# 1444 one-element memsets on GpSimd in a planned decoder-layer kernel

## The chip, the cores and the metric

The kernel runs on one core of a Trainium2 chip. The metric is the device time of one execution in microseconds (us). A core has a matrix engine (TensorE, PE in the profile, its weight loads PEld), VectorE (DVE), ScalarE (ACT), GpSimd (POOL) and SyncE (SP), which here only issues transfers. Each engine works through its own list of instructions in order and waits on semaphores for the others; 16 DMA engines move the data.

## The reference, cut to what matters

One mixer layer runs on 1024 new tokens and on 8 single tokens with stored state, at model width 2048:

```
h = rmsnorm(x) * (1 + scale(c)) + shift(c)          # modulation from w_ada
z = h @ w_in                                        # 2048 x 8208
y_a = b * conv3(c_a * h_a) * silu(g_a)              # 8 groups of 128 channels
q, k, v = silu(conv4(qkv)); q, k = l2norm(q), l2norm(k)
o = gated_delta_rule(q, k, v, g, beta, s0)          # 8 heads of 128, chunked, triangular solve
y = concat(y_a, rmsnorm(o) * silu(g_b)) @ w_out     # 2048 x 2048
out = final_rmsnorm(x + gate(c) * y)
```

The outputs also hold the new convolution and delta-rule states. The delta rule is sequential: each head's state S goes from one chunk of tokens to the next. Nothing in the reference corresponds to a memset.

## The kernel before

**Work.** The tokens go in two halves: half 0 has 512 tokens, half 1 has 512 and the 8 single ones (520 columns in two blocks). Per half, w_in is walked in 64 column tiles of 128 (32 for the eight heads, 32 for the eight convolution groups) and then w_out in 16. A tile is four splits; a split is 512 rows by 128 columns of weights, `raw`. To keep fp32 precision at the faster fp32r matmul, `split_w` (L568) makes two parts of it: `whi`, a rounded copy by ScalarE, and `wlo = raw - whi`, by GpSimd or VectorE. The activations are split likewise (`hh`, `hl`; `yhi`, `ylo` for the output projection). Each 128 rows take three matmuls per block: hh with whi, hl with whi, hh with wlo. I call these matmuls, written to the tiles `mm`, the stream; one split is 12 of them per block. `raw`, `whi` and `wlo` have four buffers each.

**Side chains.** Beside the stream runs one chain per head and half (`gdn_prep`, `gdn_invert`, `gdn_apply`): transposes `tpt`, products of k and q (`sp`), a triangular solve by VectorE in 31 steps (`ob`, `xb`) with trips through memory (`ub`, `tb`, `xd`, `yc`), and then a row of small dependent products on TensorE, with a step on VectorE or ScalarE between each and the next: `cht<-xc,dU`, `cht<-yc,pt`, `cht<-X,dU`, `cht<-Y,pb`, `cht<-v,Y`, and for each of four token chunks `cht<-u,kt`, `ot<-u,dA`, `cht<-st,kq`, `cht<-rt,Y`. I call these the chain's steps.

**What sets the order.** Python code writes out each engine's list at build time. A planner (`_Order`) keeps an estimate of when each engine is free and each tile ready; every instruction issued through the wrappers `V`, `S`, `G`, `SY` and `mm` adds to it, GpSimd memsets too (L347: a cost of 0.035 plus 0.00085 per element in the planner's own units, and a claim on a port shared with VectorE in `shared`, L146). After every stream matmul `pump` (L247) asks which chains' next step has become ready in that estimate, and writes it there. So an instruction that is added anywhere can move steps everywhere behind it. Two rules matter here. In `split_w`, a split goes to GpSimd if the planner has GpSimd free within 1.0 of now, else to VectorE. And in `head` (L1680), a new head's first tile may not start before the chain of the head before the last has finished its last chunk:

```
if part == 0:
    while recd[half] < len(queue) - 2:
        od.advance()
```

`advance` (L255) writes no stream matmul: it moves the planner on to the next chain step and writes that. What it writes stands in TensorE's list with nothing of the stream between. I call such a place a hold. (The cause is memory: `kq`, a head's k and q, has three buffers.)

The split before the change:

```
def split_w(raw, whi, wlo):
    S.activation(whi[:], raw[:], AF.Copy)
    eng = G if od.free["G"] <= od.now + 1.0 else V
    eng.tensor_tensor(wlo[:], raw[:], whi[:].bitcast(F32), ALU.subtract)
```

Nearly all instructions go through the wrapper and carry its line L321 in the profile (L370 for matmuls), so they are told apart by tile names. `spot`, new, is one element in one partition; L454 to L459 of the changed file are part of the setup, behind the memsets of `ones`, `nhalf`, `phalf` and `sc` on GpSimd and ahead of that of `wlt`.

Of the kernel before, what the change touches and what calls it, by code (L numbers as in the profile page):

```python
# [8 lines left out]
F32 = mybir.dt.float32  # L9
# [68 lines left out]
def trunk_kernel(tc, xT, w_in, w_ada, w_out, pack, consts, vecs, csq, ssm,  # L78
                 yT, cap, cqp, ssp, cas, cqs, sss):
    nc = tc.nc  # L80
    ctx = ExitStack()
    with ctx:
        _trunk(ctx, tc, nc, xT, w_in, w_ada, w_out, pack, consts, vecs, csq, ssm, yT, cap, cqp, ssp, cas, cqs, sss)
# [299 lines left out]
def _trunk(ctx, tc, nc, xT, w_in, w_ada, w_out, pack, consts, vecs, csq, ssm, yT, cap, cqp, ssp, cas, cqs, sss):  # L383
    od = _Order()
    V, S, G, SY = (_Engine(od, e, k) for e, k in ((nc.vector, "V"), (nc.scalar, "S"), (nc.gpsimd, "G"), (nc.sync, "Y")))
    mm, pump = _Tensor(od, nc.tensor).mm, od.pump

    def pool(name, bufs, stack=ctx, **kw):
        return _Pool(od, stack.enter_context(tc.tile_pool(name=name, bufs=bufs, **kw)), bufs)

    RAW, SPL, FX = 4, 4, 5
    cp = pool("cp", 1)
# [34 lines left out]
    def pkv(n, a=0, w=None):  # L427
        o, ww = PK[n]
        return pk[:, o + a:o + a + (ww if w is None else w)]

    def ck(n, a=0, w=None):
# [22 lines left out]
    V.tensor_tensor(sc[:, :, 0:9], cth[:, :144].rearrange("p (k b) -> p k b", b=9),  # L454
                    pkv("c").rearrange("p (k b) -> p k b", b=9), ALU.mult)

    held = {"ch": 0}


# [108 lines left out]
    def split_w(raw, whi, wlo):  # L568
        S.activation(whi[:], raw[:], AF.Copy)
        eng = G if od.free["G"] <= od.now + 1.0 else V  # L570
        eng.tensor_tensor(wlo[:], raw[:], whi[:].bitcast(F32), ALU.subtract)

    class Stream:

# [28 lines left out]
        def ahead(self, most=SPL):  # L603

            while True:
                if self.loaded < min(self.split + RAW, len(self.todo)):
                    raw = wp.tile([P, 4, P], F32, tag="raw", name="raw", bufs=RAW)
                    for a, b, src in self.todo[self.loaded][1]:
                        SY.dma_start(raw[:, a:b, :], src)
                    self.raws.append(raw)  # L610
                    self.loaded += 1
                elif most and self.split < min(self.freed + SPL, self.loaded) and (
                        self.eager or self.split < self.used + 2 or self.landed()):
                    whi = wp.tile([P, 4, P], F32R, tag="whi", name="whi", bufs=SPL)
                    wlo = wp.tile([P, 4, P], F32R, tag="wlo", name="wlo", bufs=SPL)
                    split_w(self.raws[self.split], whi, wlo)
                    self.raws[self.split] = None
                    self.done.append((whi, wlo))
                    self.split += 1
                    most -= 1  # L620
                else:
                    return
# [1293 lines left out]
```

## Time and profile before

| what | value |
|---|---|
| median of 3 runs | 2313.4 us (2312.58 to 2316.38) |
| the profiled execution | 2316.31 us |
| its span, first to last instruction | 2314.5 us |
| mean granted TensorE clock | 0.965 |
| TensorE busy | 2165.6 us (94%) |
| VectorE busy | 1236.9 us (53%) |
| ScalarE busy | 827.1 us (36%) |
| GpSimd busy | 827.3 us (36%), 807 instructions |

The profile is of one execution, which took 1.8 us beyond its span and 2.9 us more than the median. Times in it count from the span's start. Matmuls overlap, so a busy TensorE may still be slowed: by the granted clock, which is 1.0 or 0.5 at any moment, and shows as a mean in each stretch. A row of the timeline has start, duration, engine, line, operation, tiles written and read, shapes, count, and in brackets how long the engine stood idle before and for whom.

### The profile page before, as it was taken

Reading aid. Unit: us, or ns where it says so; the run is one execution under the profiler, and the core shown is the slowest. Engines: PE = TensorE matmul, PEld = TensorE weight load, DVE = VectorE, ACT = ScalarE, POOL = GpSimd, SP = SyncE. Lnnn points to the kernel's source line nnn. Section 1 sums busy time; section 2 is a strip of 40 time slices with the busy share of each in tenths; the row PEclk is TensorE's granted clock in tenths of the full one; section 3 lists DMA queues with packets and bytes.
Section 4 is the critical chain, followed back from the end, with each engine's and each line's share of the span. In section 5 each row is a group of like instructions: output and inputs, shape, how many; then the busy total and the mean of one; then the engine's idle time right before and its main releaser. Section 6 shows DMA issues by size and latency. Waiting matters only on the chain. (4 is left out here: it accounts for less than half of the span.)

```text
span 2314.5 us, 38944 instructions
## 1 busy us (share of the span) xinstructions
PE 2165.6 (94%) x14297; PEld 1867.5 (81%) x14297; DVE 1236.9 (53%) x3647; ACT 827.1 (36%) x1885; POOL 827.3 (36%) x807
## 2 busy tenths in 40 slices
PE   5999999897989999789999999998989999999997
PEld 2467677675868888568889999998989998898996
DVE  3355676463856662148315757655465476235545
ACT  3234243333434323133324334242433432225553
POOL 1223433333324334222434333343433342334444
PEclk8999999998979999989999999999999999999998
DMA  9965977997656667976445786679894565997776
GB/s 323 328 173 87 155 148 131 121 132 101 128 76 88 95 92 77 58 114 190 151 120 100 129 106 105 122 98 95 99 88 83 87 95 87 77 68 211 211 222 202
DMA packets 462496, 299.56 MB, mean 129 GB/s; under 512 B 37600, under 2 KB 421344, under 8 KB 462304
## 3 DMA queue, kind: packets, MB, share of 16 engines
q1 hardware_dynamic: 438512, 284.26, 71.2%
q10 hardware_dynamic: 23792, 12.81, 2.2%
q8 instruction: 112, 1.84, 0.3%
q14 instruction: 80, 0.66, 0.1%
HBM read 277.06 MB, written 19.94 MB: 128 GB/s over the span
## 5 line engine op out<-in xcount | busy, mean ns | idle before, releaser
L321 POOL TENSOR_TENSOR wlo<-raw,whi 128x512 fp32r<-128x512 f32 x535 | 710.3, 1330 | 1377.8 <-ACT whi L321 1234.8
L370 PE MATMUL mm<-hh,whi 128*128 128x264 f32 (+1 forms) x3008 | 982.1, 326 | 33.3 <-ACT whi L321 17.5
L370 PE MATMUL mm<-hh,wlo 128*128 128x264 f32 (+1 forms) x3008 | 982.2, 327 | 10.3 <-POOL wlo L321 9.3
L370 PE MATMUL mm<-hl,whi 128*128 128x264 f32 (+1 forms) x3008 | 978.2, 325 | 1.4 <-DVE hl L321 1.4
L321 ACT ACTIVATE whi<-raw 128x512 fp32r<-128x512 f32 x672 | 418.5, 628 | 769.0 <-DMA raw<-in_w_in 312.1
L370 PEld LDWEIGHTS mm<-hh,whi 128*128 128x128 f32 x3008 | 576.2, 192 | 91.2 <-ACT whi L321 23.4
L370 PEld LDWEIGHTS mm<-hh,wlo 128*128 128x128 f32 x3008 | 576.2, 192 | 63.3 <-POOL wlo L321 18.0
L370 PEld LDWEIGHTS mm<-hl,whi 128*128 128x128 f32 x3008 | 576.4, 192 | 45.0 <-issue 3.4
L370 PE MATMUL mm<-yhi,wlo 128*128 128x512 f32 (+2 forms) x768 | 250.0, 326 | 5.6 <-DVE wlo L321 4.4
L370 PE MATMUL mm<-ylo,whi 128*128 128x512 f32 (+2 forms) x768 | 249.0, 324 | 2.8 <-DVE ylo L321 2.7
L370 PE MATMUL mm<-yhi,whi 128*128 128x512 f32 (+2 forms) x768 | 248.5, 324 | 0.9 <-ACT whi L321 0.9
L321 DVE TENSOR_TENSOR ob<-tb,xb 128x62 f32<-128x62 f32 (+30 forms) x992 | 196.3, 238 | 24.3 <-DMA tb<-ub 24.2
L321 DVE TENSOR_TENSOR wlo<-raw,whi 128x512 fp32r<-128x512 f32 x137 | 105.4, 775 | 162.8 <-ACT whi L321 159.8
L321 DVE TENSOR_TENSOR xb<-xb,ob 128x62 f32<-128x62 f32 (+30 forms) x992 | 184.4, 226 | 0.0
L370 PEld LDWEIGHTS mm<-yhi,wlo 128*128 128x128 f32 x768 | 146.6, 191 | 20.0 <-DVE wlo L321 6.0
L370 PEld LDWEIGHTS mm<-ylo,whi 128*128 128x128 f32 x768 | 146.6, 191 | 16.8 <-DVE ylo L321 4.1
L370 PEld LDWEIGHTS mm<-yhi,whi 128*128 128x128 f32 x768 | 146.6, 191 | 12.6 <-ACT whi L321 1.3
L321 DVE SCALAR_TENSOR_TENSOR kq<-zr,pk,kq 128x512 f32<-128x512 f32 x96 | 100.1, 1043 | 3.4
L321 DVE SCALAR_TENSOR_TENSOR res<-mm,ga,xr 128x512 f32<-128x512 f32 (+2 forms) x48 | 27.3, 568 | 111.5 <-PE mm L370 103.8
L321 DVE TENSOR_TENSOR acc<-acc,sqt 128x512 f32<-128x512 f32 (+3 forms) x70 | 50.1, 719 | 46.8 <-ACT sqt L321 45.8
L321 DVE TENSOR_SCALAR u<-cht,sm 128x128 f32<-128x128 f32 x64 | 22.3, 348 | 71.3 <-PE cht L370 71.3
L321 DVE SCALAR_TENSOR_TENSOR rt<-cht,gt_neg,v 128x128 f32<-128x128 f32 x56 | 19.5, 349 | 67.8 <-PE cht L370 67.6
(408 smaller groups left out, 1981.8 us busy)
## 6 DMA issues: line engine op xcount, KB each, us to landing
raw<-in_w_in SPq DMA_DIRECT2D x488, 256.0 KB, 7.0
raw<-in_w_out SPq DMA_DIRECT2D x160, 256.0 KB, 3.1
wat<-in_w_ada SPq DMA_DIRECT2D x64, 512.0 KB, 7.2
gw<-in_w_ada SPq DMA_DIRECT2D x64, 256.0 KB, 7.9
tb<-ub ACTq DMA_DIRECT2D x16, 512.0 KB, 8.3
raw<-in_w_in SPq DMA_DIRECT2D x48, 128.0 KB, 6.4
sl<-in_ssm SPq DMA_DIRECT2D x12, 512.0 KB, 6.2
x1s<-in_xT SPq DMA_DIRECT2D x16, 260.0 KB, 8.1
```

The source lines that it names most:

```text
L321: r = f(*args, **kw)
L370: r = self.pe.matmul(out, lhsT, rhs, **kw)
```

## The change

The change adds a tile of one element, 100 memsets of it during setup and two more behind each of the 672 splits, all on GpSimd, 1444 in all. Nobody reads the tile. They are issued through the planner's wrapper `G`.

```
+    spot = cp.tile([1, 1], F32, name="spot")
+    for _ in range(100):
+        G.memset(spot[:], 0.0)
...
     def split_w(raw, whi, wlo):
         S.activation(whi[:], raw[:], AF.Copy)
         eng = G if od.free["G"] <= od.now + 1.0 else V
         eng.tensor_tensor(wlo[:], raw[:], whi[:].bitcast(F32), ALU.subtract)
+        for _ in range(2):
+            G.memset(spot[:], 0.0)
```

**On GpSimd.** In the rows below, from the start of GpSimd's list after the change, "waits Pool_49" is a wait on GpSimd's own semaphore: every memset of `spot` but the first waits for an earlier one of them, since they write the same element. The other waits are on transfers (DMAHW), TensorE and ScalarE.

```order
L321 MEMSET sc 128x512
L321 MEMSET spot 1x1
L321 MEMSET spot 1x1 [waits Pool_49] x99
L321 MEMSET wlt 128x96
L321 ISA
L321 TENSOR_TENSOR rsm<-rsm,nhalf 128x4 [waits DVE_49]
L321 TENSOR_TENSOR wlo<-raw,whi 128x512 [waits DMAHW7_49,DMAHW0_49,Activation_49]
L321 MEMSET spot 1x1 [waits Pool_49] x2
L321 TENSOR_TENSOR wlo<-raw,whi 128x512 [waits DMAHW2_49,DMAHW1_49,Activation_49]
L321 MEMSET spot 1x1 [waits Pool_49] x6
```

Before, the memset of `wlt` follows that of `sc` directly, and splits follow each other. Groups of four, six or eight `spot` are those of splits whose subtraction went to VectorE. GpSimd subtracts 535 splits before and 520 after, VectorE 137 and 152.

**On TensorE, in half 0.** The stream of half 0 before the output projection is counted here in matmuls to `mm`. Behind the 1760th, at the boundary between two tiles, stands a hold before the change. The numbers behind names only tell buffers apart.

```order
L370 MATMUL mm<-hl,whi 128x512
L370 MATMUL mm<-hh,wlo 128x512
L370 MATMUL cht<-X,dU 64x64 x4
L370 MATMUL cht<-Y,pb 64x64 x4
L370 MATMUL cht<-v,Y 128x128
L370 MATMUL cht<-u_6057,kt 128x128
L370 MATMUL ot<-u_6059,dA 128x128
L370 MATMUL cht<-st_165,kq 128x128 x2
L370 MATMUL cht<-rt,Y 128x128
```

So it goes on, through all four chunks of this chain and the normalisation of half 1's input (`cht<-ones,acc` and `cht<-cs,rsm`), for 21 rows, until `ot<-u_6218,dA`; only then comes the next `mm<-hh,whi`. The same chain after the change, on the same engine:

```order
L370 MATMUL cht<-X,dU 64x64 x4
L370 MATMUL tpt<-sp 128x256 x6
L370 MATMUL mm<-hh,whi 128x512
L370 MATMUL mm<-hl,whi 128x512
L370 MATMUL mm<-hh,wlo 128x512
L370 MATMUL cht<-Y,pb 64x64 x4
L370 MATMUL mm<-hh,whi 128x512
L370 MATMUL mm<-hl,whi 128x512
L370 MATMUL mm<-hh,wlo 128x512
L370 MATMUL mm<-hh,whi 128x512
L370 MATMUL mm<-hl,whi 128x512
L370 MATMUL mm<-hh,wlo 128x512
```

The chain now begins at the 1668th stream matmul instead of the 1740th (`cht<-xc,dU`), and its steps stand mostly six stream matmuls apart; only its last, an `ot<-u,dA`, still stands at the 1760th, two behind the step it depends on.

The place at the 1568th, also a tile boundary, has one step before the change (`ot<-u,dA`). After it, TensorE's list reads:

```order
L370 MATMUL mm<-hl,whi 128x512
L370 MATMUL mm<-hh,wlo 128x512
L370 MATMUL cht<-rt,Y 128x128
L370 MATMUL cht<-u_5886,kt 128x128
L370 MATMUL ot<-u_5888,dA 128x128
L370 MATMUL mm<-hh,whi 128x512
L370 MATMUL tpt<-cs,kq 128x128 x4
```

Three dependent steps stand there in a row: a short hold. Over the whole program, steps that stand nearer than about five full-width stream matmuls to the step they depend on number 29 of 248 before (13 of them in the hold at the 1760th) and 18 of 248 after. The steps of a chain elsewhere are moved by up to some 200 stream matmuls, earlier or later; TensorE has the same instructions in all, and the output projections' stream is the same. SyncE issues the same transfers, most of them at the same place or one to three loads of weights away, and at most 17 (one `dA`).

## The prediction

> **What bounds the kernel now.** I read the page's first parts, then a table of stretches, then TensorE's timeline where it stalls, then the waits.
>
> ```profile
> span 2314.5 us, 38944 instructions
> ...
> PE 2165.6 (94%) x14297; PEld 1867.5 (81%) x14297; DVE 1236.9 (53%) x3647; ACT 827.1 (36%) x1885; POOL 827.3 (36%) x807
> ...
> PEclk8999999998979999989999999999999999999998
> ```
>
> TensorE is busy for 94% of the span and GpSimd, which gets the new work, for 36%. So the question is not whether GpSimd has room (it is idle for 2314.5 - 827.3 = 1487 us) but what TensorE waits for. Its granted clock dips around the 12th slice, from 637 to 694 us. The table of stretches shows that place. Its columns are the stretch, its length, busy time and count on PE, PEld, DVE, ACT and POOL, the granted clock, the DMA engines' busy share and GB/s:
>
> ```profile
> 430.00:658.00 228.00, 211.82 (x1082) 162.76 (x1081) 134.59 (x405) 83.63 (x201) 78.16 (x79) 0.96 0.84 118
> 640.00:658.82 18.82, 18.82 (x124) 14.81 (x122) 7.85 (x13) 5.63 (x13) 7.23 (x8) 1.00 0.84 113
> 658.82:685.46 26.64, 15.48 (x69) 12.12 (x68) 18.98 (x114) 7.09 (x17) 2.71 (x6) 0.57 0.30 49
> 672.00:685.46 13.46, 9.05 (x35) 7.03 (x34) 12.07 (x96) 3.02 (x8) 1.17 (x1) 0.50 0.00 1
> 685.46:689.50 4.04, 4.04 (x14) 3.28 (x14) 4.04 (x28) 2.25 (x12) 1.31 (x1) 0.50 0.40 48
> 685.46:800.00 114.54, 113.97 (x575) 92.84 (x574) 76.00 (x242) 46.78 (x120) 45.72 (x43) 0.98 0.61 92
> 950.00:1000.00 50.00, 39.68 (x137) 27.57 (x136) 4.37 (x5) 6.94 (x11) 14.39 (x13) 0.88 0.93 59
> 1000.00:1300.00 300.00, 293.97 (x1643) 254.96 (x1642) 151.48 (x288) 110.25 (x204) 108.05 (x97) 0.98 0.56 139
> 1300.00:1600.00 300.00, 292.05 (x2513) 288.49 (x2511) 191.30 (x629) 107.13 (x269) 111.91 (x119) 0.98 0.75 108
> 1600.00:1900.00 300.00, 282.74 (x2395) 277.67 (x2396) 175.33 (x584) 107.43 (x276) 112.36 (x123) 0.97 0.73 92
> ```
>
> From 658.82 to 685.46 us TensorE does 69 matmuls in 26.64 us, at a mean clock of 0.57, and in the second half of that the loads stop altogether (DMA share 0.00). TensorE's timeline says why; the bracket is its idle time before the row and whom it waited for:
>
> ```profile
> 658.50 0.39 PE L370 MATMUL mm<-hh,wlo 128*128 128x512 f32 x1
> 658.82 0.68 PE L370 MATMUL cht<-X,dU 64*64 64x64 f32 x8
> 659.96 0.67 PE L370 MATMUL cht<-Y,pb 64*64 64x64 f32 x8 [0.47 <-ACT pb L321]
> 661.10 0.49 PE L370 MATMUL cht<-v,Y 128*128 128x128 f32 x2 [0.47 <-ACT Y L321]
> 664.52 0.79 PE L370 MATMUL cht<-u,kt 128*128 128x128 f32 x2 [2.94 <-DVE u L321]
> ...
> 682.98 0.80 PE L370 MATMUL cht<-rt,Y 128*128 128x128 f32 x2 [0.45 <-DVE rt L321]
> 684.61 0.76 PE L370 MATMUL cht<-u,kt 128*128 128x128 f32 x2 [0.84 <-DVE ob L321]
> 685.17 0.63 PE L370 MATMUL ot<-u,dA 128*128 128x128 f32 x2
> 685.46 0.77 PE L370 MATMUL mm<-hh,whi 128*128 128x512 f32 x1
> ```
>
> This is the hold behind the 1760th stream matmul. The steps run one behind the other with nothing between, each waits for VectorE or ScalarE, and the stream resumes only when the chain is through. No weights are split meanwhile, so no buffer comes free and SyncE loads nothing. Behind it TensorE is busy again for 113.97 of 114.54 us with the DMA engines at 0.61, and it stays at 98%, 97% and 94% in the three stretches from 1000 to 1900: TensorE sets the pace from there on, so time saved in the hold should reach the end.
>
> **The change, part by part.** *The hold.* After the change the chain's steps stand among the stream, mostly six matmuls apart. What remains of the 26.64 us is the steps' own work: 15.48 us busy at a clock of 0.57 is 15.48 x 0.57 = 8.8 us at full clock. So 26.64 - 8.8 = 17.8 us go. The stream also starts at half clock behind the hold, up to 689.50: of these 4.04 us half go, 2.0 us. Bounds: the waits alone, with the clock as it was, would give 26.64 - 15.48 = 11.2 us; if the steps hid entirely beside the stream's own work, it would be 26.64 + 2.0 = 28.6. I take -19.8, since the clock was 1.00 in the stretch with the stream running (640.00:658.82), and the steps do take TensorE's time.
>
> *New short spacings.* Six full-width stream matmuls last 6 x 0.23 = 1.4 us, by two neighbours in the timeline:
>
> ```profile
> 708.78 0.39 PE L370 MATMUL mm<-hh,wlo 128*128 128x512 f32 x1
> 709.01 0.40 PE L370 MATMUL mm<-hh,whi 128*128 128x512 f32 x1
> ...
> 411.52 0.49 PE L370 MATMUL ot<-u,dA 128*128 128x128 f32 x2 [1.45 <-ACT u L321]
> ```
>
> The last row is a step that stands right behind its forerunner (992nd stream matmul) before: it costs a wait of 1.45 us, as much as the spacing it lacks. Leaving out the old hold, the steps with less than about five matmuls to their forerunner lack 7.9 us of such spacing in all before (16 steps) and 12.8 us after (18 steps, the short hold at the 1568th and the step at the 1760th among them). If each lack is waited out in full, that adds 5 us, if none, 0; by the row nearest to it (1.45) most is, and I take +3.0.
>
> *The memsets themselves.* GpSimd's smallest memsets and what they follow, and what its own queue waits for:
>
> ```profile
> 0.24 0.10 POOL L1893 MEMSET const-float32-0.0<- 128x1 f32 x1 [0.24 <-issue]
> 0.27 0.10 POOL L1893 MEMSET const-float32-1.0<- 128x1 f32 x1
> ...
> 1.41 0.18 POOL L321 MEMSET wlt<- 128x96 f32 x1
> 21.34 1.01 POOL L321 TENSOR_TENSOR rsm<-rsm,nhalf 128x4 f32<-128x4 f32 x1 [19.75 <-DVE rsm L321]
> ```
>
> ```profile
> POOL wlo L321 <- ACT whi L321: 1234.8, 442, 15.5
> POOL wlo L321 <- PE mm L370: 68.2, 25, 5.8
> ...
> PE mm L370 <- POOL wlo L321: 10.2, 17, 0.8
> ```
>
> ```profile
> L321 POOL TENSOR_TENSOR wlo<-raw,whi 128x512 fp32r<-128x512 f32 x535 | 710.3, 1330 | 1377.8 <-ACT whi L321 1234.8
> ...
> L321 DVE TENSOR_TENSOR wlo<-raw,whi 128x512 fp32r<-128x512 f32 x137 | 105.4, 775 | 162.8 <-ACT whi L321 159.8
> ```
>
> A memset of one column takes 0.10 us, and two that don't wait for each other start 0.03 us apart. Those of `spot` wait for each other, so I take 0.10 to 0.15 us each: 144 to 217 us on GpSimd in all. The 100 of the setup push the last setup memset from 1.41 us to at most 1.41 + 15 = 16.4, still ahead of the power at 21.34 us (`rsm` to the -0.5), the next that anybody waits for: nothing. A pair behind a split delays only what stands next in GpSimd's list. Of its 535 splits, 442 + 25 start after an idle wait for ScalarE or TensorE, which hides the pair; at most 68 don't. TensorE waits directly for a GpSimd part 17 times, 10.2 us in all. If each of these 17 came 0.3 us later, it would be 5 us; I take +0.5, since most of them follow an idle GpSimd. A gain is excluded: nothing is taken off GpSimd by a memset.
>
> A rule speaks against this. The Trainium skill, page "SBUF — State Buffer", section "Who interferes with whom", says that GpSimd shares a pair of memory ports with VectorE and that a VectorE copy or single-input arithmetic in its fast mode holds the pair for the whole instruction and blocks GpSimd. The trace has both kinds of small GpSimd work beside the same VectorE work (durations least/median/most, in ns):
>
> ```profile
> L321 POOL COPY halo<-zr x48: 179/186/651, 166.7 to 1894.5; 128x3 f32<-128x3 f32 x48
> L321 POOL MEMSET zr<- x24: 93/100/125, 164.6 to 754.1; 128x3 f32 x24
> ```
>
> Copies stretch to 651 ns, as the rule would have it; memsets never beyond 125. By the rule a pair could take up to 1.3 us, and the sum would rise by 17 x 1.3 = 22 us at worst; by the row it doesn't, and I go by the row.
>
> *Fifteen splits from GpSimd to VectorE.* Each is finished sooner (775 ns against 1330), and VectorE gets 15 x 0.775 = 11.6 us more in 2314.5 us at 53%. Zero; bounds of 15 x 0.555 = 8 us either way.
>
> *Steps moved elsewhere, half 1 above all.* No hold of more than one step comes or goes there. TensorE is idle there for 6 + 8 + 17 = 31 us in the three stretches from 1000 to 1900, for waits of 0.3 to 4 us. I take zero, and a fifth of that, 6 us, either way.
>
> **Sum.** -17.8 - 2.0 + 3.0 + 0.5 = -16.3 us. The profiled execution took 2316.3 us (2.9 above the median), which gives 2300.0, and 2297 against the median of 2313.4. A difference below 0.2%, 4.6 us, can't be told from none here.
>
> **The rivals.**
>
> *The wait comes back at the loads: no change.* The stretch 950 to 1000 is bound by loads (DMA share 0.93, TensorE busy 39.68 of 50). If the loads set when that stretch ends, TensorE gets there 18 us earlier and waits 18 us more: 2313. Against it: the loads stood still in the hold too (0.00 in 672.00:685.46), because they wait for buffers that the stream frees, so they move forward with it. For it: the share of 0.84 from 430 to 658, which would rise by a tenth.
>
> *The pair of memsets decides: slower.* If waiting for its forerunner makes each memset cost m, GpSimd does a split in 1.33 + 2m us, and the stream takes one per 12 x 0.23 = 2.8 us in half 0. From m = 0.7 us GpSimd bounds the stream. Already at m = 0.3, if the 68 splits that start without an idle wait each held up TensorE by 0.6 us, that is +41 us, 2313 - 16 + 41 = 2338; it decides from 0.24 us of lateness for each, m = 0.12. Against it: 0.10 us a memset, and TensorE waits for GpSimd 17 times, not 68. The Trainium skill, "Advanced Engine Details and Errata", "Miscellaneous Facts", puts reading a semaphore by a sequencer at 50 to 100 ns; no run here shows that. With it, an estimate, m would be 0.15 to 0.20, and the setup's 100 would end close to the power at 21.34.
>
> *The chains wait although spread: slower or no change.* If six matmuls (1.4 us) are too few on the chip after the change, for instance since VectorE has more splits and the solve of another head in its list, 248 steps at 0.1 us are +25: 2313 - 16 + 25 = 2322. It decides from 0.066 us a step. Against it: before, nearly all steps have the same spacing, and TensorE is busy for 113.97 of 114.54 us at 685.46:800.00 with it.
>
> **How the numbers follow.** The forecast has 0.76, with 2288 (6 better in half 1, 3 from spacing) to 2309 (2 more from spacing, 4 from memsets, 6 in half 1) as its own range; the loads 0.09; the memset pair 0.06; the spread chains 0.09, half of it for each of no change and slower. Faster than 2308.8 us are the forecast and a third of the loads' case, in which only part is given back: 0.76 + 0.03 = 0.79. Within 0.2%: 0.06 + 0.045, about 0.11. Slower: 0.06 + 0.045, about 0.10. The range that leaves out 2 in 10 reaches from 2285 to 2314: below, the bounds of half 1 and of the steps' hidden work; above, the case that all is given back.
>
> **What the profile after would show.** Right: no stretch of TensorE without `mm` near 650 to 690 us; the rows from `cht<-X,dU` to `ot<-u,dA` of that chain with full-width `mm` between; the clock there near 1.0; output projection of half 0 and everything behind it earlier by 15 to 20 us; `spot` x1444 at 0.10 to 0.15 us each, GpSimd busy 827 - 15 x 1.33 + 144 to 217 = 950 to 1025 us; a wait of 1 to 3 us at the new short hold. Wrong: TensorE waiting more for `wlo` by GpSimd than 10 us in all, or `spot` rows of 0.3 us and more (the pair); more than 10 us of idle before 1000 us on `whi` (loads); or TensorE idle before `cht` and `ot` rows by some tenths of a us everywhere (spread chains).

## The result, and the profile after

| | median, us | runs |
|---|---|---|
| before | 2315.22 (2306.44 to 2321.21) | 20 |
| after | 2298.84 (2293.02 to 2315.04) | 20 |

The ratio is 0.994, 95% interval 0.9926 to 0.9954: the memsets make the kernel 0.6% faster. By the ratio that is 13.9 us (10.6 to 17.1), by the two medians 16.4; the forecast was -16.3. Two executions in the experiments, 2590.8 us of before and 4082.7 us of e7, took far longer than all others and are left out of the ratios. The kernel before measures 2304.8 to 2307.7 us on the chips of the experiments and 2315.2 here, so everything below goes by ratios to the runs of before on the same chip. Changes in us are the ratio's share of that chip's median of before.

The profiled execution after took 2307.0 us, 8 us above its median. That matters when stages are compared: a stage that is a few us longer in one profile may belong to that execution. Its first parts:

```profile
span 2305.2 us, 40366 instructions
...
PE 2154.7 (93%) x14297; PEld 1862.5 (81%) x14297; DVE 1248.9 (54%) x3662; ACT 825.7 (36%) x1885; POOL 899.4 (39%) x2236
...
PEclk8999999998999999999999999999999998999998
```

The 7 in the clock's 12th slice before is a 9 now. The hold's chain is the chain that begins with `cht<-X,dU` here (TensorE's timeline, after):

```profile
644.63 0.67 PE L370 MATMUL cht<-X,dU 64*64 64x64 f32 x8
645.24 0.97 PE L370 MATMUL tpt<-sp 128*128 128x256 f32 x6
646.05 0.40 PE L370 MATMUL mm<-hh,whi 128*128 128x512 f32 x1
...
646.83 0.68 PE L370 MATMUL cht<-Y,pb 64*64 64x64 f32 x8
647.44 0.51 PE L370 MATMUL mm<-hh,whi 128*128 128x512 f32 x1
...
648.94 0.39 PE L370 MATMUL cht<-v,Y 128*128 128x128 f32 x2
...
650.56 0.39 PE L370 MATMUL cht<-u,kt 128*128 128x128 f32 x2
...
653.24 0.49 PE L370 MATMUL ot<-u,dA 128*128 128x128 f32 x2 [0.90 <-ACT u L321]
```

No step down to `cht<-u,kt` has a wait in brackets; the 2.94 us for `u` are gone, since stream matmuls stand between. The new short hold behind the 1568th stream matmul costs one wait:

```profile
610.34 0.38 PE L370 MATMUL cht<-rt,Y 128*128 128x128 f32 x2
611.26 0.46 PE L370 MATMUL cht<-u,kt 128*128 128x128 f32 x2 [0.54 <-DVE ob L321]
611.62 0.49 PE L370 MATMUL ot<-u,dA 128*128 128x128 f32 x2
611.87 0.48 PE L370 MATMUL mm<-hh,whi 128*128 128x512 f32 x1
```

To place the rest, I cut the span at the starts of the same stream matmuls in every kernel. The table gives the time between them in one profiled execution each (e1 and e4 are experiments below: the order alone, and head 6 later).

| stream matmuls | where | before | after | e1 | e4 |
|---|---|---|---|---|---|
| to 1000 | start, half 0 | 423.9 | 422.1 | 419.2 | 426.3 |
| 1000 to 1400 | half 0 | 132.3 | 142.4 | 142.0 | 132.6 |
| 1400 to 1784 | around the hold | 137.3 | 121.0 | 121.7 | 101.0 |
| 1784 to 2700 | half 0 | 241.4 | 241.9 | 243.7 | 248.5 |
| 2700 to 2912 | bound by loads | 81.1 | 72.2 | 68.0 | 71.1 |
| 2912 to 3680 | output projection, half 0 | 183.8 | 180.7 | 180.7 | 180.5 |
| 3680 to 9888 | half 1 | 893.1 | 900.3 | 886.8 | 891.9 |
| 9888 on, up to the last stream matmul's start | output projection, half 1 | 207.4 | 210.3 | 205.2 | 207.2 |

The columns of e1 and e4 come from a chip on which before is 10 us faster, so they differ from the column of before by 33 and 41 us in all, where the runs differ by 17.5 and 29.7. Four experiments below have the order of before (e2, e3, e9 and e10) and show how far single profiles scatter: 132.8 to 137.5 us around the hold, 77.6 to 80.5 in the stretch bound by loads, and 130.7 to 132.7 from the 1000th to the 1400th (138.9 in e3, with its 5476 memsets).

Three of these stretches as windows (length, busy time and count of PE, PEld, DVE, ACT, POOL, clock, DMA share, GB/s), before and then after:

```profile
423.90:556.18 132.28, 119.44 (x593) 88.44 (x592) 65.19 (x201) 42.94 (x103) 45.70 (x45) 0.97 0.96 123
556.18:693.50 137.32, 122.83 (x617) 98.31 (x616) 93.98 (x352) 53.79 (x136) 41.18 (x46) 0.86 0.61 101
934.90:1016.01 81.11, 63.07 (x213) 43.90 (x212) 10.24 (x14) 17.62 (x31) 20.78 (x18) 0.87 0.91 64
```

```profile
422.09:564.53 142.44, 123.16 (x592) 91.86 (x590) 67.06 (x237) 43.29 (x104) 46.86 (x111) 0.92 0.93 117
564.53:685.48 120.95, 110.89 (x607) 88.34 (x606) 85.64 (x263) 50.71 (x125) 44.74 (x113) 0.96 0.68 114
927.35:999.59 72.24, 60.11 (x251) 44.70 (x250) 17.50 (x30) 20.14 (x44) 22.09 (x57) 0.95 0.90 67
```

The second row is the hold: 16.4 us less for the same stream, and the clock goes from 0.86 to 0.96. The first row is a loss of 10.2 us that I had not forecast, with the same matmuls (593 and 592). TensorE's longest waits in it, before and then after (us in total, times, longest):

```profile
PE mm L370 <- ACT whi L321: 4.2, 2, 3.7
PE tpt L370 <- DVE v L321: 2.3, 1, 2.3
PE cht L370 <- ACT Y L321: 1.5, 1, 1.5
```

```profile
PE tpt L370 <- DVE sp L321: 5.2, 1, 5.2
PE cht L370 <- ACT X L321: 4.6, 1, 4.6
PE cht L370 <- ACT evg L321: 3.0, 1, 3.0
```

After, three single waits of side chains make 12.8 us, at places where the new order asks for a result too early. But TensorE waited there before as well, elsewhere: its idle time goes from 12.8 us (132.28 - 119.44) to 19.3 (142.44 - 123.16). That is 6.4 of the 10.2 us; the other 3.7 are busy time, with the clock at 0.92 instead of 0.97. The third row is a gain that I had not forecast: 8.9 us in the stretch that loads bind. TensorE waits there less for weights, before and after:

```profile
PE mm L370 <- ACT whi L321: 12.1, 7, 3.6
PE mm L370 <- POOL wlo L321: 5.6, 10, 0.6
```

```profile
PE mm L370 <- ACT whi L321: 7.3, 5, 2.5
PE mm L370 <- POOL spot L321: 2.5, 4, 0.6
```

After the change a chain stands in this stretch (251 matmuls instead of 213), but that isn't what shortens it: e8 and e12 have 213 matmuls there, as before, and take 67.8 and 71.0 us. What goes with its length is the hold at the 1760th: it takes 77.6 to 81.1 us in the six kernels that hold 15 or 17 steps there (before, e2, e3, e6, e9, e10) and 67.8 to 73.7 in the eight others. A possible reason is that the loads stand still in the hold; no run isolates it.

GpSimd's groups after (busy us, mean ns, idle before):

```profile
L321 POOL TENSOR_TENSOR wlo<-raw,whi 128x512 fp32r<-128x512 f32 x520 | 691.0, 1329 | 1278.9 <-ACT whi L321 1227.6 <-PE mm L370 35.9 <-DVE ylo L321 9.0
L321 POOL MEMSET spot<- 1x1 f32 x1444 | 132.9, 92 | 50.2
```

On average a memset's row has (132.9 + 50.2) / 1444 = 0.127 us: 0.092 at work and 0.035 idle ahead of it. The average mixes two kinds. The first of a group starts without a wait, some 0.07 us before the split ahead of it ends. Each further one starts 0.146 us after its forerunner: 0.088 of duration and 0.058 idle, the same in e2 and e3.

One caution on such rows: "POOL spot" as the one waited for is mostly a new name. The wait for `wlo` before is put down to `spot` after, because the memset is the last thing on GpSimd ahead of the waiter's start. In the built program each split still raises GpSimd's semaphore itself.

### The profile page after: what moved, and what is told of

Same layout as the page of the kernel before. It is cut to its first block, busy times and chain, and to the rows that moved or that the text cites. A ratio compares the mean times of both kernels' runs of the same rounds, so it can differ in the third digit from the quotient of the medians.

```text
span 2305.2 us, 40366 instructions
## 1 busy us (share of the span) xinstructions
PE 2154.7 (93%) x14297; PEld 1862.5 (81%) x14297; DVE 1248.9 (54%) x3662; ACT 825.7 (36%) x1885; POOL 899.4 (39%) x2236
## 5 line engine op out<-in xcount | busy, mean ns | idle before, releaser
L321 POOL TENSOR_TENSOR wlo<-raw,whi 128x512 fp32r<-128x512 f32 x520 | 691.0, 1329 | 1278.9 <-ACT whi L321 1227.6
L370 PEld LDWEIGHTS mm<-hh,whi 128*128 128x128 f32 x3008 | 575.1, 191 | 85.3 <-ACT whi L321 14.3
L370 PEld LDWEIGHTS mm<-hh,wlo 128*128 128x128 f32 x3008 | 575.1, 191 | 52.8 <-POOL spot L321 10.1
L370 PEld LDWEIGHTS mm<-hl,whi 128*128 128x128 f32 x3008 | 575.2, 191 | 41.7 <-issue 2.5
L321 DVE TENSOR_TENSOR wlo<-raw,whi 128x512 fp32r<-128x512 f32 x152 | 111.7, 743 | 158.6 <-ACT whi L321 156.3
L321 DVE TENSOR_TENSOR xb<-xb,ob 128x62 f32<-128x62 f32 (+30 forms) x992 | 190.1, 232 | 0.0
L370 PEld LDWEIGHTS mm<-yhi,wlo 128*128 128x128 f32 x768 | 147.0, 191 | 20.1 <-DVE wlo L321 6.0
L321 POOL MEMSET spot<- 1x1 f32 x1444 | 132.9, 92 | 50.2
```

The lines of the kernel that those rows point to most:

```text
L321: r = f(*args, **kw)
L370: r = self.pe.matmul(out, lhsT, rhs, **kw)
```

## The experiments

Two questions: is it the order (a built list that happens to differ) that brings the gain, and what do the memsets cost by themselves?

### e1 and e2: the order without memsets, and memsets without the order

e1 tells the planner of the memsets and issues none; e2 issues them behind the planner's back, so that all else stands as before.

```
 e1    od.put("G", [], [spot[:]], 0.03585, True)      # in place of each G.memset(spot[:], 0.0)
 e2    nc.gpsimd.memset(spot[:], 0.0)                 # in place of each G.memset(spot[:], 0.0)
```

> The planner is told of the 1444 memsets, but none is issued: the lists of all engines are those of the change without the rows of spot. Theory (the moved order is all of it): 2298 us, within 3 us of the changed kernel (2298.8), ratio to before 0.993, no hold near 660 us. Rival A (the memsets on the chip make the difference): back at 2315, ratio 1.000. Rival B (the memsets cost something that the order pays for): 2290 to 2295.

> The 1444 memsets are issued at the same places, but the planner isn't told: the lists are those of before, plus the rows of spot. Theory: 2315 to 2317, ratio 1.000 to 1.001, the hold of 26 us there as before. Rival A: 2299. Rival B: 2318 to 2323.

Measured: e1 2287.79 us, ratio 0.9924 (0.9896 to 0.9952), -17.5 us. e2 2314.11 us, ratio 1.0033 (1.0014 to 1.0051), +7.6 us. The order is the whole gain, and the memsets take some of it back: e2's theory (1.000 to 1.001) falls and its rival B (3 to 8 us more) holds, while e1's interval alone doesn't tell its theory from its rival B. Their price is more than the half microsecond of the forecast. The changed kernel is at 0.994, 0.0016 above e1, which is some 4 us for the memsets in that order; the intervals of e1 and of the change overlap, so this is a rough figure.

### e3: four times the memsets

```
 e2, with
-        for _ in range(2):
+        for _ in range(8):
             nc.gpsimd.memset(spot[:], 0.0)
```

> As the one before, with eight memsets behind each split instead of two (5376 and the 100 of the setup), still unknown to the planner. By the rows of the changed kernel a memset that waits for the one before it takes 183 us / 1444 = 0.127 us, so eight take 1.0 us, and GpSimd does a split in 1.33 + 1.0 = 2.3 us, still under the 2.8 us that the stream takes for one in half 0. Theory (what stands behind a split is covered by GpSimd's idle time): 2315 to 2322, ratio under 1.003. Rival (GpSimd's list is close to the path, since SyncE's loads wait for its parts): each back-to-back split is 0.8 us later than with two, 50 to 68 of them, +40 to +54: 2355 to 2370.

Measured: 2347.33 us, ratio 1.0181 (1.0154 to 1.0208), +41.7 us for 5476 memsets. The theory of hidden memsets falls. The loss is as large as the rival said (+40 to +54), but not where it said: by the same cuts as above, the output projection of half 1 (9888 on) takes 226.7 us instead of 207.4, nearly half of the loss.

### e9: the eight memsets only behind the last 96 splits

```
         eng.tensor_tensor(wlo[:], raw[:], whi[:].bitcast(F32), ALU.subtract)
+        for _ in range(8 if ws.split >= 576 else 0):
+            nc.gpsimd.memset(spot[:], 0.0)
```

> The order of before; 8 memsets of one element behind each of the last 96 splits only (the output projection of half 1), given out on GpSimd without telling the planner, and none anywhere else: 768 memsets. Theory: the cost of memsets sits where TensorE asks for a split as fast as GpSimd gives one. In the output projection of half 1 a tile of one block uses up a split in 12 x 0.122 = 1.47 us; a split and its eight memsets take 1.33 + 8 x 0.127 = 2.3 us there. In the profile of the kernel with 8 behind each split this stretch was 219.9 us before and 239.5 us with them, so this kernel loses 15 to 22 us, ratio 1.0065 to 1.0095, nearly half of that kernel's +42 us for a seventh of its memsets. Rival: each memset costs the same wherever it stands: 768 / 5476 x 42 = 5.9 us, ratio 1.0026.

Measured: 2329.34 us, ratio 1.0088 (1.0055 to 1.0122), +20.3 us for 768 memsets, as the theory has it: a seventh of e3's memsets, half of its loss. (The 219.9 and 239.5 us that it names are cut at other points than the 207.4 and 226.7 here; they differ by as much.) The output projection of half 1 as a window, before and e9:

```profile
2092.88:2300.25 207.37, 200.23 (x1678) 193.37 (x1676) 110.71 (x242) 106.63 (x233) 100.61 (x77) 0.98 0.75 220
```

```profile
2088.32:2313.09 224.77, 204.62 (x1678) 195.22 (x1676) 100.69 (x241) 106.72 (x231) 166.84 (x837) 0.98 0.69 203
```

The same 1678 matmuls take 17.4 us more. TensorE's waits in the same window, before and e9:

```profile
PE mm L370 <- POOL wlo L321: 0.8, 1, 0.8
```

```profile
PE mm L370 <- POOL spot L575: 13.3, 21, 1.3
PE cht L370 <- POOL spot L575: 3.6, 1, 3.6
```

13.3 + 3.6 = 16.9 us of waiting for GpSimd, where it had been 0.8. GpSimd is busy for 167 of 225 us and still late: what counts is how often one split is asked for behind the last, not the share.

### e10: eight memsets that don't write the same element

```
+    spot = cp.tile([1, 8], F32, name="spot")
...
+        for i in range(8):
+            nc.gpsimd.memset(spot[:, i:i + 1], 0.0)
```

> The order of before; 8 memsets behind each split, not told to the planner, as in the kernel of 5476, but each of the eight writes an element of its own (no memset writes what the one ahead of it wrote), and the 100 of the setup are left out: 5376 memsets. Theory: the price of 0.127 us is that of an instruction on GpSimd, whatever it writes: again +36 to +48 us, ratio 1.0155 to 1.021, and the group of memsets shows busy time and idle time ahead as there. Rival: part of the price is the wait for the memset ahead, which writes the same element: each then takes 0.09 us or less, the eight 0.7 us or less instead of 1.0, and the time is +20 to +32 us, ratio 1.009 to 1.014.

Measured: 2314.33 us, ratio 1.003 (1.0011 to 1.005), +6.9 us. The rival is right in its direction, and goes further than it said: below its +20. The group of memsets in e3 and in e10:

```profile
L577 POOL MEMSET spot<- 1x1 f32 x5376 | 484.3, 90 | 276.3
```

```profile
L575 POOL MEMSET spot<- 1x1 f32 x5376 | 214.1, 93 | 0.0
```

Each lasts as long (90 and 93 ns), but those of elements apart overlap: 5376 of them occupy 214.1 us, 0.040 us each, against (484.3 + 276.3) / 5376 = 0.141 us. One pack of eight in each kernel, from GpSimd's timeline:

```profile
2250.77 1.11 POOL L577 MEMSET spot<- 1x1 f32 x8
2252.96 1.29 POOL L321 TENSOR_TENSOR wlo<-raw,whi 128x512 fp32r<-128x512 f32 x1 [1.07 <-ACT whi L321]
```

```profile
2246.60 0.32 POOL L575 MEMSET spot<- 1x1 f32 x8
2246.89 1.27 POOL L321 TENSOR_TENSOR wlo<-raw,whi 128x512 fp32r<-128x512 f32 x1
```

1.11 us against 0.32 us. Some seven tenths of the memsets' price, (0.141 - 0.040) / 0.141, was the wait of each for the one ahead, which writes the same element. With the memsets behind all splits, the loss goes roughly with the GpSimd time of their rows: e2 165.8 us (122.3 busy and 43.5 idle for its 1344 behind splits) for +7.6, e10 214.1 for +6.9, e3 760.6 for +41.7, which is 3 to 6% each time. In e9, where all stand in one place, it is 20.3 us for 108.8 (68.9 and 39.9), 19%: the place counts for more than the time.

### e4 and e8: the hold taken away in the table

No memset here. The table `order` says in which sequence tiles come; head 6's first tile is what waits in the hold, so it is put further back.

```
-  ... h(0, 1) + h(6) + h(0, 2) + a(4, 1, 2)
+  ... h(0, 1) + h(0, 2) + a(4, 1, 2) + h(6)              # e4: two steps held at the 992nd, two at the 1904th
+  ... h(0, 1) + a(4, 1) + h(6) + h(0, 2) + a(4, 2)       # e8: two at the 992nd, seven at the 1808th
```

> The kernel before, without any memset, with one entry of its table of tiles for half 0 moved: head 6 starts three tiles later. The hold shrinks from 17 chain steps (and seven rows of the normalisation) to two. Theory (the hold is what costs): by the old hold's 26.6 us less 8.8 of work and 2.0 of half clock behind it, 19.8 us for its 17 steps, 15 of 17 go: 2315 - 17 = 2298, with 2293 to 2304. Rival (15 splits that go to VectorE, or the spread of orders in general): nothing that ties it to the hold, 2315 or anywhere.

> The kernel before, no memset, one tile of the other group moved ahead of head 6: the hold shrinks from 17 steps to seven (and two elsewhere as before). Theory: 10 steps of 1.2 us go, 2315 - 12 = 2303, with 2298 to 2309. Rival (scatter): anywhere.

Measured: e4 2275.88 us, ratio 0.9871 (0.9844 to 0.9897), -29.7 us; e8 2291.32 us, ratio 0.9934 (0.9911 to 0.9958), -15.2 us. e4 gains more than its theory allowed (0.9905 to 0.9953 by ratio); e8 lies within its own. e4 is the fastest kernel of the study. Its stretch around the old hold (1400th to 1784th stream matmul):

```profile
558.93:659.96 101.03, 101.03 (x554) 81.55 (x552) 74.47 (x212) 43.88 (x105) 34.98 (x38) 1.00 0.69 122
```

TensorE is busy all of the time at full clock. Part of the chain's work (63 of the 617 matmuls) moved behind it, where the next stretch is 7.1 us longer: the two together take 349.6 us, 29.2 less than before. That is as much as e4 gains in the runs, but not proof that all of it arises here: in the table e4 is 12 us shorter elsewhere too, part of it the chip. e8's number is right and its place isn't: its stretch around the old hold takes 106.1 us, its next 263.9 instead of 241.4 (the seven held steps stand there, 10.5 us of them), so the two together lose 8.7 us, and the stretch bound by loads 13.3.

### e5, e6, e7: other phantom counts

The planner is told of other numbers of memsets behind each split, and none is issued, as in e1: lists with holds of other lengths.

```
-        for _ in range(2):
+        for _ in range(1):      # e5; 4 in e6, 6 in e7
             od.put("G", [], [spot[:]], 0.03585, True)
```

> No memset on the chip; the planner is told of 100 and of one behind each split instead of two. Holds in TensorE's list of half 0: six chain steps at the 752nd stream matmul and five at the 1568th, none at the 1760th; 528 splits on GpSimd. Theory (a hold's step costs 19.8 / 17 = 1.2 us): 11 steps against 19 before, 2315 - 9 = 2306, with 2300 to 2311. Rival (orders scatter, whatever their holds): anywhere from 2295 to 2330.

> As the one before, with four behind each split. Holds of three, two and fifteen steps, the last at the 1760th again; 515 splits on GpSimd. Theory: 20 steps against 19, 2316, with 2310 to 2321, and a stretch without stream matmuls of some 22 us near 660 us. Rival (more splits to VectorE make it faster): with 20 fewer on GpSimd under 2300.

> As above with six. Holds of fourteen steps at the 752nd and nine at the 1568th; 498 splits on GpSimd. Theory: 23 steps against 19, 2315 + 5 = 2320, with 2313 to 2327. Rival (splits): faster still than with four, 2290 to 2300.

Measured: e5 2297.81 us, ratio 0.9959 (0.9945 to 0.9973), -9.5 us, as the theory had it in number. e6 2300.78 us, 0.9972 (0.9954 to 0.9989), -6.5 us, where the theory said +1: a miss. e7 2302.94 us, 0.9986 (0.9969 to 1.0002), -3.2 us, where the theory said +5 (-2 to +12): just below its range, and not to be told from no change. The rival of the splits falls: both are slower than it said, and e7, with the most splits on VectorE, is the slowest of the three.

The profiles say that e5's number is in part luck. Without a hold at the 1760th, its stretch around that place (1400 to 1784) is as long as before, 137.5 us against 137.3: the five steps at the 1568th take 6.9 us, and chain steps that stand apart wait as well, 16.9 us of idle time in all. Its gain shows in the stretch bound by loads (70.0 us) instead. e6 has its hold where the theory had it, 20.1 us long, and its stretch takes 143.0 us; its gain shows in half 1 (875.9 us instead of 893.1).

### e11 and e12: is there more?

```
 e11   the edit of e1 and that of e4
 e12   ... h(0, 1) + h(0, 2) + a(4, 1, 2) + h(0, 3) + h(6) + ...     # head 6 behind head 0's last tile too
```

> Both orders in one: the planner is told of the 1444 memsets and none is given out (alone: ratio 0.9924), and head 6 of half 0 stands behind chunk 4's last tiles in the table (alone: 0.9871). The built order has one hold of 3 steps, at the 1568th matmul of the stream. Theory: both gains are the same one, the stretch of some 19 chain steps during which the stream stands still, so they don't add: 3 steps held, as in the order alone and one fewer than with the table alone, ratio 0.985 to 0.993. Rival: the two gains come from different places and add: 0.9924 x 0.9871 = 0.9796, so 0.976 to 0.983.

> No memset; head 6 of half 0 one step further back in the table than in the kernel with head 6 behind chunk 4's last tiles (ratio 0.9871): behind the last tile of head 0 too. The built order has a single hold, of 2 steps, at the 992nd matmul of the stream, where the other has two of 2 steps. Theory: what is left of the hold sets the time, and there are 2 steps fewer to lose: as that kernel or up to 4 us faster, ratio 0.984 to 0.988. Rival: head 6 now comes so late that its chain ends behind the loads of the last tiles and delays what waits for it: 5 to 15 us slower than that kernel, ratio 0.989 to 0.994.

Measured: e11 2284.05 us, ratio 0.9906 (0.9874 to 0.9939), -21.7 us: the gains don't add, as they shouldn't if it is the same hold. Its profile has e4's gain around the hold in part (109.2 us) and also the loss of after and e1 in the stretch from 1000 to 1400 (141.8). e12 2288.45 us, 0.9918 (0.9896 to 0.9939), -18.9 us: the theory that only the held steps count falls, the rival holds. From the 1784th to the 2700th stream matmul e12 takes 262.2 us where e4 takes 248.5, since head 6's late chain stands there:

```profile
659.96:908.50 248.54, 244.39 (x1281) 197.41 (x1279) 149.41 (x519) 89.42 (x214) 98.96 (x92) 1.00 0.71 91
```

```profile
655.53:917.75 262.22, 254.25 (x1316) 205.49 (x1315) 153.81 (x532) 92.39 (x229) 99.93 (x96) 0.97 0.68 86
```

The first row is e4, the second e12: TensorE is idle for 4.2 us in the one and 8.0 in the other, and does 35 more matmuls at a lower clock.

All orders without memsets, by the steps that stand in holds of two steps and more:

| kernel | steps held | change, us |
|---|---|---|
| before | 17 + 2 | 0 |
| e7 | 14 + 9 | -3.2 |
| e6 | 3 + 2 + 15 | -6.5 |
| e5 | 6 + 5 | -9.5 |
| e8 | 2 + 7 | -15.2 |
| e1 | 3 | -17.5 |
| e12 | 2 | -18.9 |
| e11 | 3 | -21.7 |
| e4 | 2 + 2 | -29.7 |

Fewer held steps, less time, in the rough: the three kernels with 19 to 23 stand at the top, those with two to four at the bottom. But steps aren't all that counts. e7's two holds take 31.3 us, longer than the 26.6 of before, and e7 isn't slower; kernels with two to four differ by 12 us. The rest presumably lies where else an order makes TensorE wait; no run takes that apart.

## Why the prediction was right, point by point

The direction, the cause (the order, by way of the hold) and the size of the sum were right. That the sum came within 3 us is in part luck: several terms that I had at nothing or nearly so were larger and cancel, as the points below say.

*The hold (-19.8) and the new short spacings (+3.0).* Right in place and mechanism; as close in size as the profiles can tell. The stretch around it is 16.4 us shorter, against -16.8 forecast, where the kernels with the order of before scatter by 5 us; the clock there went up as said, and the order alone (e1) measures -17.5 (-24.0 to -11.1). e4 shows that this was not all there was: with nearly no hold the stretch and the one behind it lose about 29 us together (25 to 29 against the other kernels with the order of before), about the upper bound of 28.6 that I gave the hold. What after keeps in the stretch is a wait of 5.5 us and one of 1.5 in the normalisation of half 1's input, which stood in the old hold and is now a hold of its own. The forecast had it go among the stream with the rest. So by e4 -19.8 was too little for the whole hold, and 6.7 us of one stayed. The waits and TensorE's timeline (after, 655 to 685 us):

```profile
PE cht L370 <- DVE rsm L321: 5.5, 1, 5.5
PE cht L370 <- DVE acc L321: 1.5, 1, 1.5
```

```profile
674.80 1.05 PE L370 MATMUL cht<-ones,acc 128*128 128x1 f32 x8 [1.53 <-DVE acc L321]
681.35 0.20 PE L370 MATMUL cht<-ones,acc 128*8 128x1 f32 x2 [5.49 <-DVE rsm L321]
681.48 0.79 PE L370 MATMUL mm<-hh,whi 128*128 128x512 f32 x1
```

What the short spacings cost was not taken apart; the profile shows 0.5 us at the new short hold and 0.9 at the chain's first `ot<-u,dA`.

*The memsets (+0.5, bounds 0 to 5).* Mis-sized. The price of one, 0.10 to 0.15 us, was right (0.127 on average, 0.146 behind its forerunner), and so was the setup: its 100 end at 16.08 us, and the power still waits for VectorE, not for them:

```profile
1.40 14.68 POOL L321 MEMSET spot<- 1x1 f32 x100
16.02 0.18 POOL L321 MEMSET wlt<- 128x96 f32 x1
21.19 1.01 POOL L321 TENSOR_TENSOR rsm<-rsm,nhalf 128x4 f32<-128x4 f32 x1 [4.99 <-DVE rsm L321]
```

What failed is the step "a pair behind a split delays only what stands next", counted on 17 direct waits of TensorE: e2 measures +7.6 us (3.2 to 11.8) for them in the order before, and in the order after it is some 4. I took the stream's pace from half 0 alone, 2.8 us for a split. In the output projection of half 1 a tile of one block takes 1.47 us for one, and there a longer GpSimd is felt at once (e9: 17 us with eight). With two behind each split that stretch is no longer than before (206.5 us in e2's profile), so e2's own 7.6 us lie elsewhere. Its profile shows 388.3 us instead of 382.3 from the first to the 1000th stream matmul, and e3's and e10's show 385.4 and 387.0; where in it GpSimd is late was not settled.

*The signs I named.* Not all came. The output projection of half 0 begins at 999.6 us instead of 1016.0, 16.4 earlier (15 to 20 named), but what stands behind it doesn't keep that: the output projection of half 1 begins 12.3 us earlier, and the span ends 9.3 earlier. A stretch without `mm` is left, the 6.7 us just shown, and the clock from 655 to 690 us is 0.85 (0.61 before), not near 1.0. The new short hold costs 0.54 us, less than the 1 to 3 named. TensorE waits for GpSimd's parts less than 10 us in all, as said. Its idle time on `whi` before 1000 us is 9.9 us, just under the 10 named; before it was 14.3, so that sign could tell nothing.

*GpSimd's busy time.* Forecast 950 to 1025 us, measured 899.4. The forecast took the memsets' time as added to the rest. But the rows of the memsets make 132.9 us and all others 808.5, 941.4 together, and GpSimd is busy for 899.4: 42 us overlap, the first memset of each group with the split ahead of it. And the waits between them, 50.2 us, aren't counted as busy.

*Fifteen splits to VectorE (0).* 520 and 152 as built; VectorE is 12.0 us busier (1248.9 against 1236.9). No run isolates it.

*Steps moved elsewhere (0, bounds of 6 us).* Zero was right as a sum and wrong in its parts. I looked for them in half 1; the two large ones are in half 0, +10.2 us from the 1000th to the 1400th and -8.9 us in the stretch bound by loads, and they nearly cancel, which is luck. Both come with the order: e1 has them too (+9.7, -13.1). The second goes with the hold, as said above, so it was probably a part of the hold's worth that I left out. In half 1, after is 7.2 us longer than before and e1 6.3 shorter; e2, e9 and e10, whose lists there differ from those of before by memsets at most, are between 0.3 shorter and 5.1 longer, so nothing can be said of single profiles at that size.

*The rival of the loads.* Refuted, in a way I had not thought of: the stretch that loads bind got shorter (81.1 to 72.2 us), as in all kernels without the hold at the 1760th, and nothing of the gain came back as waiting for weights.

*The rival of the memset pair.* The direction holds, the size doesn't: a price of 0.127 us lies just above the m = 0.12 that I named for the pair to decide, and yet the kernel is faster. The 68 splits that I let each hold up TensorE didn't: its waits for GpSimd's parts are 6.4 us in all after, 10.2 before. With eight memsets, e3, a late GpSimd does make the kernel slower, and nearly half of that in the last stretch.

*The rival of the spread chains.* In part: single waits of 5.2, 4.6 and 3.0 us where a result is asked for too early, not some tenths at each of 248 steps.

*The rule on ports.* After, 21 of the 1444 memsets last over 125 ns and the longest 382:

```profile
L321 POOL MEMSET spot<- x1444: 88/88/382, 1.4 to 2289.7; 1x1 f32 x181
```

I had said "never beyond 125". The rule of the Trainium skill, "SBUF — State Buffer", "Who interferes with whom", would put it down to VectorE; no run here shows what stretches these few, and nothing like 1.3 us a pair shows. The other statement of the Trainium skill that I weighed, "Advanced Engine Details and Errata", "Miscellaneous Facts" (50 to 100 ns to read a semaphore), now has rows: behind its forerunner a memset starts after 58 ns of idle time, in after as in e3, and the 100 of the setup take 14.68 us, 0.147 each with a duration of 0.088. That agrees, near the lower end, if this idle time is that reading. My estimate from it, 0.15 to 0.20 us, fits at its lower end; the average of 0.127 is less because the first of each group doesn't wait.

## What to carry to other kernels

When a planner writes the order, a change that does nothing can still move the time by a per cent: separate the two by telling the planner without issuing (e1) and issuing without telling (e2). Then fix what the accident pointed at: here one entry of a table (e4) gives twice the gain of 1444 memsets. And judge work on a half-idle engine at the place where it is asked most often, not by its share of the span.

## What the runs showed of the hardware

Small GpSimd memsets overlap unless they depend on each other: 0.040 us each for elements apart (e10), 0.141 us for the same element (e3), at 93 and 90 ns of duration. One that waits for its forerunner starts 58 ns after that one has ended. And long waits of TensorE came with a lower granted clock: 1.00 over 101 us without a wait in e4, 0.96 and 0.86 in the same part of the stream after and before, where TensorE was idle for 10.1 and 14.5 us. It isn't the sum of the idle time alone: before has 11.2 of its 14.5 us within the hold of 26.6 us, while e5 has 16.9 us there, in no gap of the stream longer than 6.9 us, at 0.93.
